# Later feed-forwards of a two-layer decoder trunk: a second pair of column groups through seven products, and another order of the matmuls in a group

## The chip, the cores and the metric

The kernel runs on one core of a Trainium2 chip, in one launch. The metric is the device time of a run in microseconds (us). One run of each kernel is taken by the hardware profiler; its span is the time from the first to the last instruction of the core, and the run's own time is a little longer than that.

## The reference, cut to what matters

Two layers work on 256 tokens of width 1024 in float32. Each layer is: a feed-forward, a token mixer, a second feed-forward, each followed by a layer norm. So there are four feed-forwards in all; the change is about these.

```python
def swiglu(x, w_gate, w_up, w_down):
    return (jax.nn.silu(x @ w_gate) * (x @ w_up)) @ w_down
...
D_FF = ((8 * D_MODEL // 3 + 127) // 128) * 128        # 2816
...
x = layer_norm(ALPHA * x + 0.5 * swiglu(x, ffn1_gate[l], ffn1_up[l], ffn1_down[l]), ln_g[l, 0], ln_b[l, 0])
```

## The kernel before, in words

**Precision.** Every float32 operand is split into a high part, rounded to the chip's fp32r type, and a low part, the rest. A product of two operands is three matmuls (high by high, high by low, low by high), which the helper `mm3` issues (line 120). A weight tile is 128 x 1024 (512 KB). It is loaded by one DMA on SyncE's (SP's) queue into a buffer named `raw`, of which there are five. ScalarE (ACT) casts it to `wh` (line 124), then VectorE (DVE) subtracts to get `wl` (line 125). Down-projection tiles go the same way and are called `dh`, `dl`. Gate and up tiles have eight buffers for `wh` and eight for `wl`; down tiles have six of each.

**Groups.** The 2816 hidden columns are cut into eleven groups, 0 to 10, of 256 gate and 256 up columns. A feed-forward is a hand-written list of steps (`FIRST` for the first feed-forward, `ORDER` for the three later ones), and TensorE (PE) works through it in that order:

- `G g.h`: group g for token half h; the tokens stand still in the array, and the weights stream through it. The product then has to be transposed on PE, by `T` (line 647), before it can be an operand of the down projection.
- `T g` in the list is the method `GT`: a *turned* group. The weights stand still and the tokens of both halves stream, 512 columns against `wh` (high and low tokens together) and 256 against `wl`, 64 matmuls (line 528). The result comes out already transposed. It needs four PSUM banks: two column blocks, each with a gate and an up bank. `gate_turned` adds the two sums of each bank and takes silu and product (lines 553 to 557).
- `D g.h`: the down projection of group g for token half h, 12 matmuls into `acc`.
- `A g.n` and `B g.n`, n = 0 to 3: a *summed pair*, groups g and g+1 with both token halves, as a two-by-two block product with seven products in place of eight (the Strassen-Winograd scheme). It needs sums of token blocks, `Sh` and `Sl`, made once per feed-forward, and sums of weight blocks: `first_sums` (line 237) and `later_sums` (lines 242 to 245) work in place on the `raw` tiles on DVE before they are split. A pair takes 14 weight tiles, where two turned groups take eight. After the last `B`, lines 481 to 493 make the four results u, p5, v (and c11, which is ready after `A`) on ACT and DVE, and each has to be transposed by `T`.

**What sets the order around the change.** PE's order is that of the program. ACT, DVE and SP orders are set by a scheduler; ops under `high_priority` move ahead. A small clock, `later`, counts products (three matmuls of 512 columns are one tick) and puts a transposition into PE's program after a number of ticks: those of a pair 5, 8, 10 and 11 ticks after its last `B` (`TURNS`). A `GT` and an `A g.0` begin with

```python
later.wait(lambda: not self.pending)
```

which issues all transpositions that are still pending at once, ahead of the group. PSUM banks named `gu` are four in all, shared by groups, pairs and transpositions in turn; where a turned group goes *by block* (`by_block`), its first eight k-steps write two banks only, and the other two are touched 16 matmuls later.

Of the kernel before, what the change touches and what calls it, by code (L numbers as in the profile page):

```python
# [19 lines left out]
S = 256  # L20
DEPTH = 2
KT = D // P
# [19 lines left out]
FIRST, ORDER = ([(STEPS[s[0]], *(int(n) for n in s[1:].split("."))) for s in steps.split()] for steps in (  # L42
# [4 lines left out]
FINAL = [s[1] for s in ORDER if s[0] == "D" and s[2] == 0][-3:-1]  # L47
SUMMED = 40
TURNS = (5,8,10,11)
PINNED, STARTED = 4, 4  # L50
HT = 8
# [34 lines left out]
def trunk(ctx: ExitStack, tc: tile.TileContext, t, out: bass.AP):  # L86
# [13 lines left out]
    later = Later()  # L100
# [17 lines left out]
    def mm3(ps, lh, ll, wh, wl, start, stop, more=False):  # L118
        for n, (a, b) in enumerate(((lh, wh), (lh, wl), (ll, wh))):
            nc.tensor.matmul(ps, a, b, start=start and n == 0, stop=stop and n == 2, skip_group_check=more)  # L120
        later.tick()

    def halves(dst_h, dst_l, src):
        first = nc.scalar.copy(dst_h, src)  # L124
        return first, nc.vector.tensor_tensor(dst_l, src, dst_h.bitcast(F32), ALU.subtract)  # L125
# [85 lines left out]
    def full_part(n, part, pt=None):  # L211

        own = scope[0].tile([P, 4, P], F32, name="cb", bufs=4)
        if pt:
            nc.scalar.copy(own, pt)
        else:
            ks = slice(4 * part, 4 * part + 4)
            nc.vector.tensor_tensor(own, xth[:, n, ks].bitcast(F32), xtl[:, n, ks].bitcast(F32), ALU.add)
        parts_seen[n, part] = own
        if len(parts_seen) == 1:  # L220
            sums[0] = [scope[0].tile([P, 4, KT // 2, P], F32R, name="S" + n) for n in "hl"]
        if (1 - n, part) in parts_seen:
            (a11, a12), (a21, a22) = ([parts_seen[i, part][:, k::2] for k in range(2)] for i in range(2))
            raw = rawp.tile([P, 4, 2, P], F32, name="raw")
            for dst, a, b, op in ((0, a21, a22, ALU.add), (2, a11, a21, ALU.subtract), (1, raw[:, 0], a11, ALU.subtract),
                                  (3, a12, raw[:, 1], ALU.subtract)):
                nc.vector.tensor_tensor(raw[:, dst], a, b, op)
            sh, sl = (s[:, :, 2 * part:2 * part + 2] for s in sums[0])
            halves(sh, sl, raw)
        if len(parts_seen) == 4:  # L230
            parts_seen.clear()
# [121 lines left out]
    class FFN:  # L353
# [155 lines left out]
        def GT(self, g):  # L509

            later.wait(lambda: not self.pending)
            ps = [[psg.tile([P, 2 * S], F32, name="gu") for _ in range(2)] for _ in range(2)]
            n = 0
            for lo in range(2):
                w = S if lo else 2 * S

                blocks = [[0], [1]] if lo or self.by_block(g) else [[0, 1]]
                for block in blocks:  # L520
                    for kt in range(KT):
                        later.wait(lambda: min(xT[0].done, xT[1].done) > kt)
                        weight = self.gw[g][kt // 2]
                        for i in block:
                            for part in range(2):
                                c = (kt % 2) * 512 + part * GW + i * P
                                x = xt2[:, kt].rearrange("p l h t -> p (l h t)")
                                nc.tensor.matmul(ps[i][part][:, 2 * S - w:], weight.parts[lo][:, c:c + P], x[:, 0:w],  # L528
                                                 start=kt == 0 and not lo, stop=kt == KT - 1 and lo == 1)
                                n += w  # L530
                                if n >= 3 * 512:
                                    n -= 3 * 512
                                    later.tick()
                        if kt % 2 and lo and block == [1]:
                            weight.uses = 1
                            weight.used()
                    if lo:
                        self.gate_turned(g, block[0], ps[block[0]])

        def by_block(self, g):  # L540
            return g == 8 or g == 2 and not self.first

        def turned(self, g):
            return (0 if self.first else 2) <= g < NG - 1 and not {g, g - 1} & self.pairs
# [30 lines left out]
        def start(self):  # L575
# [62 lines left out]
            for i in range(2):  # L638
                self.gate_turned(0, i, ps[i])
            for n in range(4):  # L640
                later(SUMMED + 4 * n, lambda n=n: full_part(n % 2, n // 2))
            self.GT(1)

        def T(self, g, hf, hn):
# [519 lines left out]
```

## Time and profile before

| what | value |
|---|---|
| three timed runs | 941.34, 943.33, 944.40 us (median 943.33) |
| the profiled execution: its own time, its span | 944.05 us, 942.3 us |
| PE matmul busy, PE weight load busy | 930.6 us (99%), 789.9 us (84%) |
| DVE busy, ACT busy | 742.5 us (79%), 545.9 us (58%) |
| the DMA queue of SP, share of 16 engines | 59.3% |
| granted TensorE clock over the span | 0.998 |

The profiled execution is 0.7 us over the median. A busy matmul includes time in the pipeline: one of 512 columns is shown as about 0.39 us, while the next one starts 0.23 us later. So PE's speed is read from starts, or from the chain of waits, whose pieces follow each other; a group of 64 matmuls is one piece there.

### The profile page before, as it was taken

How to read it: one execution, taken by the hardware profiler on the slowest of the kernel's cores; microseconds unless marked ns; L12 is line 12 of the kernel's file. 1: busy time of each engine (PE TensorE's matmuls, PEld its weight loads, DVE VectorE, ACT ScalarE, POOL GpSimd, SP SyncE). 2: the span in 40 equal slices, each digit the busy share in tenths (PEclk: the TensorE clock that was granted, in tenths of full speed). 3: DMA queues.
4: the chain of work that ended last, by engine and by line, in shares of the span. 5: the costliest groups of instructions: out<-in, count | busy, mean ns of one | idle time of the engine just before them, and what ended most of it. 6: DMA issues, size and time to landing. Idle time of an engine off the chain costs nothing.

```text
span 942.3 us, 13155 instructions
## 1 busy us (share of the span) xinstructions
PE 930.6 (99%) x4767; PEld 789.9 (84%) x4767; DVE 742.5 (79%) x1209; ACT 545.9 (58%) x840; POOL 23.0 (2%) x38
## 2 busy tenths in 40 slices
PE   9999999999999999999999999999999999999996
PEld 7878788888988888888888888888898888888885
DVE  7787978779979768986776589947899797689825
ACT  7765667368446754765446556743975466556720
POOL 0000000010010000000000000000000000000000
PEclk9999999999999999999999999999999999999999
DMA  8855798534525765897327568953417357469801
GB/s 303 317 197 167 261 344 290 194 99 135 207 85 194 270 207 180 288 320 237 128 97 248 175 210 307 329 208 101 139 63 268 111 191 251 167 217 310 317 1 45
DMA packets 55424, 192.62 MB, mean 204 GB/s; under 512 B 6592, under 2 KB 6848, under 8 KB 55360
## 3 DMA queue, kind: packets, MB, share of 16 engines
q1 hardware_dynamic: 55024, 191.14, 59.3%
q8 instruction: 37, 0.61, 0.3%
q0 software_dynamic: 192, 0.53, 0.2%
q14 instruction: 27, 0.22, 0.1%
q10 hardware_dynamic: 144, 0.13, 0.0%
HBM read 190.72 MB, written 1.05 MB: 204 GB/s over the span
## 4 chain that ended last, share of the span: by engine, by line
PE 83%; DVE 7%; DMA 7%; issue 2%; ACT 1%; SPq 0%; DVEq 0%; ACTq 0%
PE gu L120 26%; PE acc L120 26%; PE gu L528 23%; DMA raw<-in_gu 4%; DVE wl L125 2%; PE gu L1002 2%; DMA raw<-in_dn 2%; PE acc L928 1%; PE gu L202 1%; PE acc L874 1%; PE gu L647 1%; DVE hn L556 1%; DMA raw<-in_first 1%; DVE sil L554 0%; ACT wh L124 0%
## 5 line engine op out<-in xcount | busy, mean ns | idle before, releaser
L124 ACT CAST wh<-raw 128x1024 fp32r<-128x1024 f32 x252 | 263.4, 1053 | 169.0 <-DMA raw<-in_gu 61.0
L125 DVE TENSOR_TENSOR wl<-raw,wh 128x1024 fp32r<-128x1024 f32 x252 | 303.7, 1220 | 46.1 <-ACT wh L124 24.1
L120 PE MATMUL gu<-wh,xt 128*128 128x512 f32 x672 | 221.8, 393 | 0.0
L528 PE MATMUL gu<-xt,wh 128*128 128x512 f32 x800 | 187.2, 391 | 1.5 <-DVE sil L554 0.9
L528 PEld LDWEIGHTS gu<-xt,wh 128*128 128x128 f32 x800 | 149.7, 188 | 35.0 <-DVE htl L125 1.5
L120 PEld LDWEIGHTS gu<-wh,xt 128*128 128x128 f32 x672 | 126.0, 188 | 26.4 <-DVE xt L125 0.5
L120 PE MATMUL acc<-dh,hth 128*128 128x512 f32 x354 | 140.2, 396 | 0.0
L120 PE MATMUL acc<-dh,htl 128*128 128x512 f32 x354 | 138.1, 390 | 0.0
L120 PE MATMUL acc<-dl,hth 128*128 128x512 f32 x354 | 137.5, 388 | 0.0
L120 PE MATMUL gu<-wl,xt 128*128 128x512 f32 x336 | 131.1, 390 | 0.0
L125 DVE TENSOR_TENSOR dl<-raw,dh 128x1024 fp32r<-128x1024 f32 x88 | 105.7, 1219 | 23.8 <-ACT dh L124 23.5
L124 ACT CAST dh<-raw 128x1024 fp32r<-128x1024 f32 x88 | 92.0, 1051 | 36.1 <-DMA raw<-in_dn 32.3
L528 PEld LDWEIGHTS gu<-xt,wl 128*128 128x128 f32 x800 | 99.3, 192 | 2.0
L528 PE MATMUL gu<-xt,wl 128*128 128x256 f32 x800 | 99.8, 283 | 0.0
L120 PEld LDWEIGHTS acc<-dh,htl 128*128 128x128 f32 x354 | 66.4, 188 | 14.2
L120 PEld LDWEIGHTS acc<-dl,hth 128*128 128x128 f32 x354 | 66.6, 188 | 12.1
L120 PEld LDWEIGHTS acc<-dh,hth 128*128 128x128 f32 x354 | 66.6, 188 | 11.8
L120 PEld LDWEIGHTS gu<-wl,xt 128*128 128x128 f32 x336 | 63.2, 188 | 12.7
L554 DVE TENSOR_TENSOR sil<-gu,sil 128x256 f32<-128x256 f32 x50 | 20.9, 418 | 37.3 <-ACT sil L553 37.3
L564 ACT ACTIVATE sil<-gu 128x256 f32<-128x256 f32 x20 | 7.7, 383 | 41.7 <-PE gu L120 41.5
L124 ACT CAST hth<-hn 128x256 fp32r<-128x256 f32 x52 | 21.0, 406 | 16.7 <-DVE hn L556 16.0
L314 POOL TENSOR_TENSOR rs<-rs,neghalf 128x1 f32<-128x1 f32 x11 | 10.4, 949 | 741.9 <-DVE rs L313 741.9
(206 smaller groups left out, 1042.9 us busy)
## 6 DMA issues: line engine op xcount, KB each, us to landing
raw<-in_gu SPq DMA_DIRECT2D x196, 512.0 KB, 4.8
raw<-in_dn SPq DMA_DIRECT2D x88, 512.0 KB, 4.7
raw<-in_win SPq DMA_DIRECT2D x40, 512.0 KB, 4.5
raw<-in_wout SPq DMA_DIRECT2D x16, 512.0 KB, 5.0
lng<-in_ln_g SPq DMA_DIRECT2D x6, 512.0 KB, 6.7
lnb<-in_ln_b SPq DMA_DIRECT2D x6, 512.0 KB, 7.6
x<-in_first SPq DMA_DIRECT2D x4, 384.0 KB, 3.7
raw<-in_first SPq DMA_DIRECT2D x4, 384.0 KB, 5.8
```

The costliest lines, as they stand in the source:

```text
L120: nc.tensor.matmul(ps, a, b, start=start and n == 0, stop=stop and n == 2, skip_group_check=more)
L124: first = nc.scalar.copy(dst_h, src)
L125: return first, nc.vector.tensor_tensor(dst_l, src, dst_h.bitcast(F32), ALU.subtract)
L202: nc.tensor.transpose(pt[:, k - a, :], self.nat[:, k * P:(k + 1) * P], ident)
L314: nc.gpsimd.tensor_tensor(rs, rs, neghalf[:, 0:1], ALU.pow)
L528: nc.tensor.matmul(ps[i][part][:, 2 * S - w:], weight.parts[lo][:, c:c + P], x[:, 0:w], start=kt == 0 and not lo, stop=kt == KT - 1 and lo ...
L554: nc.vector.tensor_tensor(dst, p[:, 0:S], dst, ALU.add)
L556: nc.vector.tensor_tensor(h, h, gate, ALU.mult)
L647: nc.tensor.transpose(pt[:, i, :], hn[:, i * P:(i + 1) * P], ident)
L874: nc.tensor.matmul(pe[:, a:], lf[hf][c][:, h * P:(h + 1) * P], cumM[:, c, a:], start=True, stop=True)
L928: nc.tensor.matmul(dst[:, 2 * j:2 * j + 2, :], side[:, j, :], E[:, 2 * j:2 * j + 2, t0:t0 + dst.shape[2]], start=True, stop=True)
L1002: nc.tensor.matmul(ps[i // 2][:, i % 2, :], w, x, start=kt == 0 and n == 0 and i % 2 == 0, stop=kt == KT - 1 and n == 2 and i % 2 == 1)
```

## The change

In the three later feed-forwards, groups 6 and 7 were a summed pair and 5, 8 and 9 were turned. Now 5 and 6 are a pair and 8 and 9 are a second one, and 7 is turned and goes by block. Of the turned groups that do not go by block, the order of the 64 matmuls is new: the first four k-steps with `wh`, the same four with `wl`, then the other four with `wh` (all for both blocks), and last the other four with `wl`, block by block. Before, it was all eight with `wh`, then `wl` by block. In the first feed-forward the list of steps is the same, but its turned groups take the new order too, group 8 does not go by block any more, and the token sums are asked for later (66 ticks and every 6, before 40 and every 4).

```diff
-    "G0.0 G1.0 G0.1 G1.1 D0.0 D0.1 T2 D1.0 T3 D1.1 T4 D2.0 T5 D2.1 "
-    "A6.0 A6.1 A6.2 A6.3 D3.0 B6.0 D3.1 B6.1 D4.0 B6.2 B6.3 D4.1 D5.0 D5.1 T8 D6.0 D6.1 T9 D7.0 D7.1 D8.0 G10.0 D9.0 D10.0 G10.1 "))
+    "G0.0 G1.0 G0.1 G1.1 D0.0 D0.1 T2 D1.0 T3 D1.1 T4 D2.0 "
+    "A5.0 A5.1 A5.2 A5.3 D2.1 B5.0 D3.0 B5.1 D3.1 B5.2 B5.3 D4.0 D4.1 T7 D5.0 "
+    "A8.0 A8.1 A8.2 A8.3 D5.1 B8.0 D6.0 B8.1 D6.1 B8.2 B8.3 D7.0 D7.1 G10.0 D8.0 D9.0 D10.0 G10.1 "))
...
-SUMMED = 40
+SUMMED = 66
+EARLY = 4
...
-            for lo in range(2):
-                w = S if lo else 2 * S
-
-                blocks = [[0], [1]] if lo or self.by_block(g) else [[0, 1]]
-                for block in blocks:
-                    for kt in range(KT):
+            if self.by_block(g):
+                turns = [(lo, [i], 0, KT) for lo in range(2) for i in range(2)]
+            else:
+                turns = [(lo, [0, 1], 0, EARLY) for lo in range(2)] + [(0, [0, 1], EARLY, KT)]
+                turns += [(1, [i], EARLY, KT) for i in range(2)]
+            for lo, block, first, end in turns:
...
-                        if kt % 2 and lo and block == [1]:
+                        if kt % 2 and lo and 1 in block:
                             weight.uses = 1
                             weight.used()
-                    if lo:
+                    if lo and end == KT:
                         self.gate_turned(g, block[0], ps[block[0]])
 
         def by_block(self, g):
-            return g == 8 or g == 2 and not self.first
+            return g == 7 or g == 2 and not self.first
...
-                later(SUMMED + 4 * n, lambda n=n: full_part(n % 2, n // 2))
+                later(SUMMED + 6 * n, lambda n=n: full_part(n % 2, n // 2))
```

Three places of the built programs show what moves. Names carry the buffer number of the program; line numbers of the changed kernel are 2 to 4 higher.

The first place is PE in the last feed-forward, from the pair's last transpositions (`ident`) to the turned group behind it. Before, with pair 6 and 7 and group 8 (`acc` rows are down projections):

```order
L647 MATMUL gu_8650<-ident_88,cb_8425 128x128 x2
L120 MATMUL acc_7753<-dh_8413,hth_8225 128x512
L120 MATMUL acc_7753<-dl_8414,hth_8225 128x512
L120 MATMUL acc_7753<-dh_8413,htl_8226 128x512
L647 MATMUL gu_8660<-ident_88,cb_8582 128x128 x2
L120 MATMUL acc_7753<-dh_8419,hth_8294 128x512
L120 MATMUL acc_7753<-dl_8420,hth_8294 128x512
L120 MATMUL acc_7753<-dh_8419,htl_8295 128x512
L528 MATMUL gu_8682<-xt_86,wh_8455 128x512
```

Now, with pair 5 and 6 and group 7, where `cb_8449`, `cb_8295` and `cb_8450` are u, p5 and v:

```order
L122 MATMUL acc_7763<-dh_8289,hth_8176 128x512
L122 MATMUL acc_7763<-dl_8290,hth_8176 128x512
L122 MATMUL acc_7763<-dh_8289,htl_8177 128x512
L651 MATMUL gu_8497<-ident_88,cb_8449 128x128 x2
L651 MATMUL gu_8504<-ident_88,cb_8295 128x128 x2
L651 MATMUL gu_8511<-ident_88,cb_8450 128x128 x2
L532 MATMUL gu_8518<-xt_86,wh_8325 128x512
L532 MATMUL gu_8519<-xt_86,wh_8325 128x512
```

Three down projections stood between the pair and the turned group, now two; the last two transpositions, which the clock had put 10 and 11 ticks behind the pair, now stand directly ahead of the group, 8 ticks behind it.

The second place is DVE around the same results: `cb` is u, v and p5 at lines 484 to 487 and their products with silu at line 498. Before:

```order
L125 TENSOR_TENSOR wl_8492<-raw_8490,wh_8491 128x1024
L484 TENSOR_TENSOR cb_8582<-cb_8581,gu_8443 128x512
L485 TENSOR_TENSOR cb_8581<-cb_8581,gu_8318 128x512
L486 TENSOR_TENSOR cb_8425<-cb_8425,cb_8582 128x512
L125 TENSOR_TENSOR wl_8501<-raw_8499,wh_8500 128x1024
L498 TENSOR_TENSOR cb_8581<-cb_8581 128x256
L498 TENSOR_TENSOR cb_8425<-cb_8425 128x256
L487 TENSOR_TENSOR cb_8582<-cb_8582,gu_8444 128x512
L125 TENSOR_TENSOR dl_8507<-raw_8505,dh_8506 128x1024
L498 TENSOR_TENSOR cb_8582<-cb_8582 128x256
```

Now (lines 486 to 489 and 500):

```order
L486 TENSOR_TENSOR cb_8450<-cb_8449,gu_8313 128x512
L127 TENSOR_TENSOR dl_8383<-raw_8381,dh_8382 128x1024
L487 TENSOR_TENSOR cb_8449<-cb_8449,gu_8200 128x512
L488 TENSOR_TENSOR cb_8295<-cb_8295,cb_8450 128x512
L127 TENSOR_TENSOR wl_8410<-raw_8408,wh_8409 128x1024
L500 TENSOR_TENSOR cb_8449<-cb_8449 128x256
L500 TENSOR_TENSOR cb_8295<-cb_8295 128x256
L489 TENSOR_TENSOR cb_8450<-cb_8450,gu_8314 128x512
L127 TENSOR_TENSOR htl_8485<-gu_8481,hth_8484 128x256
L127 TENSOR_TENSOR wl_8419<-raw_8417,wh_8418 128x1024
L500 TENSOR_TENSOR cb_8450<-cb_8450 128x256
L239 TENSOR_TENSOR raw_8432<-raw_8432,raw_8408 128x512
```

Between the first of these results and the last product there stood two subtractions of weight tiles, now three, and the first transposition's `htl` besides.

The third place is PE in the first feed-forward at group 8. Before, by block, the group's 14th to 18th matmul:

```order
L528 MATMUL gu_1447<-xt_86,wh_1247 128x512
L528 MATMUL gu_1446<-xt_86,wh_1247 128x512
L528 MATMUL gu_1447<-xt_86,wh_1247 128x512
L528 MATMUL gu_1448<-xt_86,wh_1202 128x512
L528 MATMUL gu_1449<-xt_86,wh_1202 128x512
```

Now the last matmul ahead of the group and its first four:

```order
L122 MATMUL acc_483<-dh_1166,htl_1042 128x512
L532 MATMUL gu_1446<-xt_86,wh_1202 128x512
L532 MATMUL gu_1447<-xt_86,wh_1202 128x512
L532 MATMUL gu_1448<-xt_86,wh_1202 128x512
L532 MATMUL gu_1449<-xt_86,wh_1202 128x512
```

The banks `gu_1448` and `gu_1449`, which were first written by the 17th and 18th matmul, are now written by the third and fourth.

More of the change, by code (lines that the diff above doesn't have):

```diff
@@ L515, in GT @@
             n = 0
-            for lo in range(2):
-                w = S if lo else 2 * S
-                blocks = [[0], [1]] if lo or self.by_block(g) else [[0, 1]]
-                for block in blocks:
-                    for kt in range(KT):
+            if self.by_block(g):
[4 more added lines that the diff above has]
+            for lo, block, first, end in turns:
+                    w = S if lo else 2 * S
+                    for kt in range(first, end):
                         later.wait(lambda: min(xT[0].done, xT[1].done) > kt)
```

## The prediction

> **What bounds the kernel now.** I read the page's totals first, then the chain of waits, then the timelines of PE, VectorE and ScalarE around one summed pair.
>
> ```profile
> span 942.3 us, 13155 instructions
> PE 930.6 (99%) x4767; PEld 789.9 (84%) x4767; DVE 742.5 (79%) x1209; ACT 545.9 (58%) x840; POOL 23.0 (2%) x38
> PE 83%; DVE 7%; DMA 7%; issue 2%; ACT 1%; SPq 0%; DVEq 0%; ACTq 0%
> ```
>
> The chain runs on PE for 83% of the span. Its pieces in the last feed-forward (start, length, what):
>
> ```profile
> 822.58 11.11 PE gu L528 x64
> 833.69 2.74 PE acc L120 x12
> 836.43 8.19 PE gu L120 x36
> ...
> 847.37 2.77 PE gu L120 x12
> ...
> 852.89 2.75 PE gu L120 x12
> ...
> 858.40 5.47 PE gu L120 x24
> 863.87 3.43 PE acc L120 x15
> 867.30 0.22 PE gu L647 x2
> ...
> 872.06 0.22 PE gu L647 x2
> ```
>
> A turned group is 11.11 us, one D is 2.74, the four A steps are 8.19, the four B steps 2.77 + 2.75 + 5.47 = 10.99, one transposition 0.22. Piece follows piece: PE loses nothing here, so what leaves PE's list leaves the time, as long as its operands keep coming.
>
> **The PE work that goes.** Groups 8 and 9 turned cost 2 x 11.11 = 22.22 us. As a pair they cost 8.19 + 10.99 = 19.18, and four transpositions 4 x 0.22 = 0.88: 20.06 together. That saves 2.16 us in a feed-forward, 6.5 in three. Moving the first pair from 6 and 7 to 5 and 6 changes no count, and the new order inside a turned group issues the same 64 matmuls.
>
> **The work that comes on other engines.** VectorE's groups in that feed-forward (busy us, mean ns), and two stretches:
>
> ```profile
> L125 DVE TENSOR_TENSOR wl<-raw,wh 128x1024 fp32r<-128x1024 f32 x37 | 44.6, 1218 | 2.0 <-ACT wh L124 1.9
> L242 DVE TENSOR_TENSOR raw<-raw 128x512 f32<-128x512 f32 x4 | 2.7, 683 | 0.0
> L237 DVE TENSOR_TENSOR raw<-raw 128x512 f32<-128x512 f32 x4 | 2.6, 683 | 1.1 <-issue 1.1
> 836.00:873.00 37.00, 37.00 (x167) 30.18 (x166) 35.27 (x47) 22.90 (x31) 0.00 (x0) 1.00 0.84 283
> sum 128.00, PE 128.00 PEld 109.29 DVE 96.34 ACT 74.98 POOL 0.00; mean PE 42.67 PEld 36.43 DVE 32.11 ACT 24.99 POOL 0.00
> ```
>
> A second pair loads 14 tiles for 8. VectorE gets 6 x 1.22 = 7.3 us of subtractions and 16 weight sums of 0.68 = 10.9; the pair's own adds and products are about what two turned groups took. That is 18 us in each later feed-forward, 96.3 to about 114 of the 126 us that PE needs there. ScalarE gets six casts, 6.3 us, and SP six more DMAs; both have room (75 of 128 us; a DMA share of 0.84 at its highest). I cost the 18 us at nothing, because PE covers it. But in the stretch of the existing pair VectorE was busy 35.3 of 37 us (the fourth column). The cover there is thin, and that is where I look for the new wait.
>
> **The new wait.** Only two D steps now stand between the first pair and group 7. Count from the end of the pair's last B, which is the start of the next D:
>
> ```profile
> 863.71 0.39 PE L120 MATMUL acc<-dh,hth 128*128 128x512 f32 x1
> ...
> 871.90 0.38 PE L647 MATMUL gu<-ident,cb 128*128 128x128 f32 x2
> ...
> 872.81 0.39 PE L528 MATMUL gu<-xt,wh 128*128 128x512 f32 x1
> ```
>
> Before, the last transposition (of v) began 8.2 us after the pair. Now PE reaches it after 2 x 2.74 and three transpositions of 0.22, at 6.1 us. When is v's product there? VectorE's rows (start, length, what; in brackets its idle time and what ended it):
>
> ```profile
> 846.32 0.69 DVE L453 TENSOR_TENSOR cb<-cb,gu 128x512 f32<-128x512 f32 x1 [0.27 <-ACT cb L452]
> 847.27 1.22 DVE L125 TENSOR_TENSOR wl<-raw,wh 128x1024 fp32r<-128x1024 f32 x1 [0.26 <-ACT wh L124]
> ...
> 861.05 2.51 DVE L125 TENSOR_TENSOR wl<-raw,wh 128x1024 fp32r<-128x1024 f32 x2 [0.55 <-ACT wh L124]
> 863.99 1.23 DVE L125 TENSOR_TENSOR wl<-raw,wh 128x1024 fp32r<-128x1024 f32 x1 [0.42 <-ACT wh L124]
> 865.13 0.68 DVE L484 TENSOR_TENSOR cb<-cb,gu 128x512 f32<-128x512 f32 x1
> ...
> 867.12 1.22 DVE L125 TENSOR_TENSOR wl<-raw,wh 128x1024 fp32r<-128x1024 f32 x1
> ...
> 869.52 1.22 DVE L125 TENSOR_TENSOR dl<-raw,dh 128x1024 fp32r<-128x1024 f32 x1
> 870.66 0.42 DVE L498 TENSOR_TENSOR cb<-cb 128x256 f32<-128x256 f32 x1
> ```
>
> It ended at 870.66 + 0.42 = 871.08, 7.4 us after the pair, and nobody waited. The same in the second feed-forward, whose first transposition begins 15 matmuls (3.43 us) after the pair:
>
> ```profile
> 402.55 0.38 PE L647 MATMUL gu<-ident,cb 128*128 128x128 f32 x2
> 405.25 0.42 DVE L498 TENSOR_TENSOR cb<-cb 128x256 f32<-128x256 f32 x1 [0.45 <-ACT cb L497]
> ```
>
> 405.67 - 399.12 = 6.55 us. After the change the same product stands behind other subtractions. In the stream of tiles the first of the pair's A is number 1, and v's product follows number 25 before and number 26 now. Six of these were through VectorE when the turned group ahead of the pair ended; now I take seven, because the new order is through with that group's first two `wl` tiles after 5.6 of its 11.1 us, not in the last quarter, so that two more tiles of A can pass; one down tile fewer stands ahead. Nineteen remain both times, with the same sums in between: by work alone 7.4 us again, plus the `htl` that now stands ahead (as long as line 498's row, 0.42), 7.8. Below that, the idle rows above (0.27, 0.26, 0.55, 0.42) can close up, since two tiles are ahead: 6.3. I take 6.5, nearest to the second feed-forward's row, since the buffers are freed in time there as well. Then PE waits 6.5 + 0.1 - 6.1 = 0.5 us for v. Behind it the second matmul of group 7 needs the bank of the second transposition, which VectorE empties after one more sum (line 237, 0.68) and one `htl`, 1.1 us after v; PE would be there 0.6 us after v: another 0.5. So 1.0 us for each later feed-forward, 3.0 in all, from 0.8 x 3 at 6.3 to 2.3 x 3 at 7.8.
>
> The second pair has G10.0 behind its two D steps, so its transpositions keep their ticks; VectorE's list there has two subtractions between the first result and v's product, as before. I cost its wait at nothing; the cover is 8.2 against 7.4 us, and were it gone, the price is the difference. The moved loads of the layer norm's gains (1 MB on SP's queue) go behind the third tile of the next A; the tiles that v waits for are issued ahead of them, so nothing.
>
> **The first feed-forward.** Its PE work is unchanged. Two waits change:
>
> ```profile
> 62.90 1.29 PE L528 MATMUL gu<-xt,wh 128*128 128x512 f32 x4 [0.91 <-DVE sil L554]
> 58.37 1.22 DVE L125 TENSOR_TENSOR Sl<-raw,Sh 128x1024 fp32r<-128x1024 f32 x1
> 62.43 0.42 DVE L554 TENSOR_TENSOR sil<-gu,sil 128x256 f32<-128x256 f32 x1
> 127.43 1.11 PE L528 MATMUL gu<-xt,wh 128*128 128x512 f32 x4
> 127.95 0.75 DVE L125 TENSOR_TENSOR htl<-gu,hth 128x256 fp32r<-128x256 f32 x2
> 129.17 0.17 DVE L720 COPY pr<-lbs 128x8 f32<-128x8 f32 x1 [0.47 <-DMA lbs<-in_lb]
> ```
>
> At 62.90 group 4 waited 0.91 us for a bank that VectorE emptied late, behind the token sums (`Sl`). Half of these now come after that emptying: I take 0.5 saved, of 0 to 0.9. At 127.43 group 8 began while two transposition banks were full until 128.70; its third and fourth matmul, at 127.89 and 128.12, now write these: 0.6 us lost. The small copies that wait for `lbs` now stand ahead of these two rows, which could make it 2.4; the DMA is issued earlier too, so I stay at 0.6.
>
> **The sum.** -6.5 + 3.0 - 0.5 + 0.6 = -3.4 us. On the profiled execution's own 944.05 that is 940.6; on the median of 943.33 it is 939.9, 0.36% less, and I give 939.9. A difference under 0.3%, 2.8 us, can hardly be told from none in runs of this kernel.
>
> [...] The page's row has PE matmul 99% and weight load 84% busy. [...]
>
> **The rivals.**
>
> First, all hidden: v comes in time everywhere and group 7 waits 0.3 us for its bank; the rest as above. -6.5 + 0.9 + 0.1 = -5.5: 937.8. For it: VectorE's idle rows may close altogether. Against: 6.1 us is under every time that v took.
>
> Second, the wait eats the gain: v at 7.8 to 8.3. Then 2.3 to 2.8 us each: 6.9 to 8.4 less 6.4, +0.5 to +2.0, so 943.8 to 945.3. For it: the count by work alone gives 7.8. Against: the second feed-forward's 6.55.
>
> Third, slower: VectorE's stream becomes the bound. A tile's round through one of five `raw` buffers:
>
> ```profile
> raw<-in_gu SPq DMA_DIRECT2D x33, 512.0 KB, 4.7
> 861.25 1.05 ACT L124 CAST wh<-raw 128x1024 fp32r<-128x1024 f32 x1 [0.23 <-DMA raw<-in_gu]
> ```
>
> 4.7 to land, 1.05 to cast, 1.22 to subtract: 7.0 us for five tiles, 1.4 each. If the two tiles are not ahead, because the buffers and not the work set VectorE's pace, v comes 2 x 1.4 later than 7.4, at 10.2. The wait is then 4.2 + 0.5 in three places: 14.1 - 6.4 = +7.7, 951. It decides against the change as soon as v takes over 7.6 us, where the wait passes 2.16. Against it: the lead is in the order of the matmuls, and the DMA has room.
>
> **How the numbers follow.** The forecast has 0.45 (938 to 942), all hidden 0.15 (935.5 to 938), the gain eaten 0.25 (942 to 945.5), the stream as the bound 0.15 (946 to 951). Faster by over 0.3% means under 940.5: three quarters of the first (0.34) and all of the second, 0.49. Slower means over 946.2: 0.15. The rest is 0.36. The range leaves out the slow case and the outermost of the hidden one: 936 to 946.
>
> **What would show it.** After the change the chain should have pieces of 8.19 and about 11 us twice in each later feed-forward, and four pieces of 11.11 where there were six. Ahead of group 7 PE should show idle time ended by DVE at line 500, and at the group's second matmul by `htl`; over 2 us there would prove me wrong towards no gain. The last product should end about 6.5 us after the pair. Group 8 of the first feed-forward should wait 0.6 us at its third or fourth matmul. Waits for `wl` inside A or B would mean the third rival.

## The result, and the profile after

| | before | after |
|---|---|---|
| median of the runs | 942.92 us (4 runs) | 951.11 us (4 runs, 949.17 to 954.76) |
| ratio after to before | | 1.0089, 95% interval 1.0071 to 1.0107 |
| the profiled execution: its own time, its span | 944.05, 942.3 us | 951.94, 950.1 us |
| granted TensorE clock over the span | 0.998 | 0.995 |

The change made the kernel 8 us slower; 3.4 us faster was forecast. The page of after, totals and chain:

```profile
span 950.1 us, 13018 instructions
PE 930.1 (98%) x4659; PEld 781.9 (82%) x4659; DVE 794.2 (84%) x1266; ACT 558.9 (59%) x843; POOL 23.1 (2%) x38
PE 66%; DVE 17%; DMA 9%; issue 4%; ACT 3%; SPq 0%; DVEq 0%; ACTq 0%
```

The matmuls are fewer (4659 for 4767), VectorE has 51.7 us more (54 were counted), and the chain of waits runs on PE for 66% of the span where it was 83%. What PE waits for (line waited for: us in all, times, longest), before and then after (one row of 1.1 us for a tile `zero`, the same in both, and the smallest rows are left out):

```profile
PE gu L528 <- DVE sil L554: 0.9, 1, 0.9
PE gu L528 <- DVE htl L125: 0.4, 1, 0.4
```

```profile
PE gu L651 <- DVE cb L500: 4.5, 9, 1.2
PE gu L651 <- DVE hn L569: 4.2, 3, 2.0
PE gu L532 <- DVE sil L558: 0.8, 1, 0.8
PE gu L532 <- DVE htl L127: 0.8, 3, 0.3
```

Two new rows carry the loss: the pairs' products (line 500), and three times the product of G10.0 (line 569). Idle time in these rows begins at the end that the profile shows for a matmul (0.39 us behind its start, where the next one can start 0.23 behind), so it is about 0.17 us short each time (the wait of 2.04 us in the rows below is 2.21 by the starts on both sides). I therefore also count **lost spacing** from the starts of all matmuls: from one start to the next, what goes beyond 0.2285 us (512 columns), 0.119 (256) or 0.1 (128), other widths in proportion to 512 (the median spacings of before are 0.227, 0.120 and 0.109), summed over the span with its sign. It is 13.2 us before and 28.0 after. Without it the two spans are 929.0 and 922.2: PE's work fell by 6.9 us, and lost spacing rose by 14.7.

PE's rows at the second pair's transpositions of the second feed-forward, and at the first pair's last one and the turned group behind it in the last feed-forward:

```profile
437.40 0.38 PE L651 MATMUL gu<-ident,cb 128*128 128x128 f32 x2
441.12 0.44 PE L651 MATMUL gu<-ident,cb 128*128 128x128 f32 x2 [1.24 <-DVE cb L500]
443.19 0.44 PE L651 MATMUL gu<-ident,cb 128*128 128x128 f32 x2 [0.24 <-DVE cb L500]
451.43 0.44 PE L651 MATMUL gu<-ident,hn 128*128 128x128 f32 x2 [2.04 <-DVE hn L569]
...
863.57 0.44 PE L651 MATMUL gu<-ident,cb 128*128 128x128 f32 x2 [0.35 <-DVE cb L500]
864.50 1.88 PE L532 MATMUL gu<-xt,wh 128*128 128x512 f32 x7 [0.26 <-DVE htl L127]
```

By start spacing, the places cost in the three feed-forwards, in order: first pair and group 7 0.86, 1.88, 1.03 (3.8 us in all); second pair and G10.0 4.02, 2.73, 1.72 (8.5 us). With 1.5 us at a low clock, shown below, and 0.5 us less in the first feed-forward that is -6.9 + 3.8 + 8.5 + 1.5 - 0.5 = 6.4 of the 7.9 us between the spans; the rest is in many small differences. Times from the end of the last B, read from PE's and VectorE's rows:

| us after the pair | u's product | v's product | PE gets to u, v |
|---|---|---|---|
| before, pair 6 and 7 | 3.61, 5.10, 4.96 | 6.56, 7.50, 7.37 | 5.70, 8.19 |
| after, pair 5 and 6 | 3.68, 4.69, 3.85 | 6.41, 7.42, 6.59 | 5.70, 6.1 |
| after, pair 8 and 9 | 7.09, 6.03, 6.43 | 9.50, 8.44, 8.83 | 5.70, 8.2 |

Why the second pair is late stands in VectorE's rows of the last feed-forward, whose second pair ends at 905.66 (the row of 919.03 is ScalarE's):

```profile
906.31 2.52 DVE L127 TENSOR_TENSOR wl<-raw,wh 128x1024 fp32r<-128x1024 f32 x2 [0.58 <-ACT wh L126]
908.74 0.68 DVE L486 TENSOR_TENSOR cb<-cb,gu 128x512 f32<-128x512 f32 x1
909.34 1.22 DVE L127 TENSOR_TENSOR dl<-raw,dh 128x1024 fp32r<-128x1024 f32 x1
910.47 0.68 DVE L487 TENSOR_TENSOR cb<-cb,gu 128x512 f32<-128x512 f32 x1
...
912.60 1.22 DVE L127 TENSOR_TENSOR dl<-raw,dh 128x1024 fp32r<-128x1024 f32 x1
913.74 0.76 DVE L500 TENSOR_TENSOR cb<-cb 128x256 f32<-128x256 f32 x2
...
918.00 2.36 DVE L127 TENSOR_TENSOR dl<-raw,dh 128x1024 fp32r<-128x1024 f32 x2
919.03 0.38 ACT L568 ACTIVATE sil<-gu 128x256 f32<-128x256 f32 x1 [1.94 <-PE gu L122]
920.27 0.42 DVE L569 TENSOR_TENSOR hn<-sil,gu 128x256 f32<-128x256 f32 x1
```

The first result (line 486) begins 3.1 us after the pair; before, its like began 1.4 after (865.13 less 863.71). In the two feed-forwards ahead of this one it begins 3.7 and 2.7 us after the second pair, and before 0.1 and 1.6 after the pair. Two subtractions for group 10 stand ahead of it in the queue, and they came late themselves (0.58 idle for ScalarE's cast). At the end the product of G10.0 could begin at 919.4, when ScalarE's silu ended, and the two subtractions of D10's tiles in row 918.00, which nobody needs yet, hold it to 920.27.

A last part of the loss is the clock. PE (first figure behind the length) and its granted clock (third from the right) in the wait at 451, behind it, and later:

```profile
449.00:451.40 2.40, 0.39 (x2) 0.00 (x0) 1.92 (x4) 1.81 (x3) 0.00 (x0) 1.00 0.96 326
453.30:456.30 3.00, 3.00 (x9) 2.36 (x8) 1.90 (x2) 1.05 (x1) 0.00 (x0) 0.51 0.99 340
457.00:460.00 3.00, 3.00 (x15) 2.46 (x14) 0.94 (x2) 0.00 (x0) 0.00 (x0) 1.00 0.77 292
```

From 452.8 on, 1.4 us behind the end of the wait, the clock is at half for 3.4 us, and eight matmuls stand 0.43 us apart: 1.5 us lost on top of the wait.

### The profile page after: what moved, and what is told of

It is laid out like the page before. It is cut to its first block, busy times and chain, and to the rows that moved or that the text cites. A ratio compares the mean times of both kernels' runs of the same rounds, so it can differ in the third digit from the quotient of the medians.

```text
span 950.1 us, 13018 instructions
## 1 busy us (share of the span) xinstructions
PE 930.1 (98%) x4659; PEld 781.9 (82%) x4659; DVE 794.2 (84%) x1266; ACT 558.9 (59%) x843; POOL 23.1 (2%) x38
## 4 chain that ended last, share of the span: by engine, by line
PE 66%; DVE 17%; DMA 9%; issue 4%; ACT 3%; SPq 0%; DVEq 0%; ACTq 0%
PE gu L122 23%; PE acc L122 19%; PE gu L532 16%; DMA raw<-in_gu 7%; DVE wl L127 6%; DVE dl L127 3%; PE gu L1006 2%; ACT wh L126 1%; DMA raw<-in_dn 1%; PE acc L932 1%; DVE raw L247 1%; DVE htl L127 1%; PE gu L204 1%; PE acc L878 1%; DVE cb L500 1%
## 5 line engine op out<-in xcount | busy, mean ns | idle before, releaser
L126 ACT CAST wh<-raw 128x1024 fp32r<-128x1024 f32 x270 | 280.6, 1053 | 191.6 <-DMA raw<-in_gu 52.0
L127 DVE TENSOR_TENSOR wl<-raw,wh 128x1024 fp32r<-128x1024 f32 x270 | 325.4, 1222 | 41.9 <-ACT wh L126 30.5
L122 PE MATMUL gu<-wh,xt 128*128 128x512 f32 x744 | 249.8, 394 | 0.0
L532 PE MATMUL gu<-xt,wh 128*128 128x512 f32 x608 | 145.8, 392 | 1.8 <-DVE sil L558 0.8
L532 PEld LDWEIGHTS gu<-xt,wh 128*128 128x128 f32 x608 | 112.8, 188 | 26.9 <-DVE sil L558 1.8
L532 PEld LDWEIGHTS gu<-xt,wl 128*128 128x128 f32 x608 | 77.2, 191 | 2.5
L532 PE MATMUL gu<-xt,wl 128*128 128x256 f32 x608 | 77.9, 283 | 0.0
L122 PE MATMUL gu<-wl,Sh 128*128 128x512 f32 x112 | 43.8, 391 | 0.0
L122 PE MATMUL gu<-wh,Sh 128*128 128x512 f32 x112 | 43.8, 391 | 0.0
L122 PE MATMUL gu<-wh,Sl 128*128 128x512 f32 x112 | 43.6, 390 | 0.0
```

## The experiments

Theories at the start: *volume*, VectorE's work is the bound around the pairs; *cover*, the work fits but the transpositions stand too close behind a pair; later a third, *order*, the results stand behind subtractions in VectorE's queue that nobody needs yet. Ratios are to runs of before on the same chip; "lost" is the lost spacing of the profiled run (before 13.2, after 28.0), "DVE" VectorE's busy time there. The edits are shortened: `...` and comments stand for code that is left out.

| run | median us | ratio (95%) | lost | DVE |
|---|---|---|---|---|
| e1 old step list, rest new | 948.59 | 1.0054 (1.0038, 1.0071) | 17.3 | 743.3 |
| e2 new step list, rest old | 954.40 | 1.0123 (1.0105, 1.0141) | 31.4 | 793.3 |
| e3 second pair turned later | 953.15 | 1.0102 (1.0089, 1.0115) | 29.7 | 794.0 |
| e4 no sums, second pair | 947.35 | 1.0044 (1.0027, 1.0061) | 19.8 | 765.5 |
| e5 sums on GpSimd | 978.65 | 1.0369 (1.0355, 1.0382) | 55.1 | 780.0 |
| e6 six raw buffers | 957.33 | 1.0146 (1.0133, 1.0159) | 31.1 | 791.2 |
| e7 pairs farther apart | 955.00 | 1.0122 (1.0107, 1.0137) | 28.2 | 793.5 |
| e8 the same, more cover | 954.69 | 1.0113 (1.0091, 1.0134) | 33.3 | 792.9 |
| e9 results first | 954.09 | 1.0118 (1.0101, 1.0134) | 29.2 | 792.9 |
| e10 e9, banks by ScalarE | 952.06 | 1.0092 (1.0074, 1.0110) | 26.6 | 792.8 |
| e11 first feed-forward only | 942.41 | 0.9991 (0.9982, 1.0000) | 11.1 | 742.4 |
| e12 no sums in the later ones | 940.90 | 0.9973 (0.9963, 0.9983) | 17.9 | 737.7 |
| e13 e1, banks by ScalarE | 944.04 | 1.0012 (1.0003, 1.0021) | 12.8 | 743.9 |
| e14 pair 5 and 6 alone | 948.78 | 1.0058 (1.0045, 1.0070) | 18.0 | 742.7 |
| e15 e10, six raw buffers | 954.99 | 1.0146 (1.0120, 1.0172) | 28.3 | 790.7 |
| e16 all results first | 945.12 | 1.0027 (1.0011, 1.0043) | 23.4 | 791.8 |
| e17 e16, G10.0 turned later | 942.97 | 1.0008 (0.9990, 1.0026) | 19.2 | 791.6 |
| e18 e17, D9's tiles ahead | 945.07 | 1.0018 (1.0003, 1.0032) | 19.3 | 791.7 |

**The parts of the change: e1, e2, e11, e14, e13.**

e1, after with the old `ORDER` (and `by_block` for group 8 of the later feed-forwards, as that list needs):

```diff
-    "... T4 D2.0 A5.0 ... D4.1 T7 D5.0 A8.0 ... D7.1 G10.0 D8.0 D9.0 D10.0 G10.1 "
+    "... T5 D2.1 A6.0 ... D4.1 D5.0 D5.1 T8 D6.0 D6.1 T9 D7.0 D7.1 D8.0 G10.0 D9.0 D10.0 G10.1 "
```

> The step list of before (one pair, 6 and 7), with everything else of the change: the new order in the turned groups, group 8 of the first feed-forward not by block, the later token sums. Volume theory (VectorE's stream of two pairs is too long for the places where PE waits for it) and cover theory (the stream fits, but the transpositions stand too close behind the pair): both 942 to 943.5, as before, since both put the loss on the second pair. Third possibility, the loss is in the new order inside the groups: 946 or more.

5 us slower without any second pair, which the third possibility had and neither theory. VectorE's rows, and PE's at group 8 of the third feed-forward:

```profile
590.53 0.42 DVE L126 TENSOR_TENSOR htl<-gu,hth 128x256 fp32r<-128x256 f32 x1
590.87 2.35 DVE L126 TENSOR_TENSOR wl<-raw,wh 128x1024 fp32r<-128x1024 f32 x2
593.13 0.41 DVE L126 TENSOR_TENSOR htl<-gu,hth 128x256 fp32r<-128x256 f32 x1
```

```profile
593.60 3.74 PE L531 MATMUL gu<-xt,wh 128*128 128x512 f32 x15 [1.57 <-DVE htl L126]
```

Two subtractions of the tiles that the new order lets in earlier stand between two `htl`, and PE waits 1.6 us for the bank that the second `htl` empties.

e2, after with the old order of matmuls in a group, and the old sums and group 8 in the first feed-forward:

```diff
-                turns = [(lo, [0, 1], 0, EARLY) for lo in range(2)] + [(0, [0, 1], EARLY, KT)]
-                turns += [(1, [i], EARLY, KT) for i in range(2)]
+            turns = ... [(0, [0, 1], 0, KT)]
+            turns += [(1, [i], 0, KT) for i in range(2)]
...
-SUMMED = 66
+SUMMED = 40
...
```

> The new step list alone: turned groups in the old order, sums and group 8 of the first feed-forward as before. Both theories: about 951, and up to 1.4 us more in each later feed-forward if the early release of two tiles had helped the pair, so 951 to 955. If the new order inside the groups costs the time: 944 to 946.

As expected, 954.4. With two pairs the new order helps (3.3 us between the medians, of which the first feed-forward's part, in this run as before, is some 0.9 by e11), but it moves the wait more than it takes it: the places at group 7 cost 9.1 us here (3.8 in after), those at the second pair 3.3 (8.5).

e11, e1 with the old order of matmuls in the later feed-forwards too:

```diff
-            if self.by_block(g):
-                turns = [(lo, [i], 0, KT) for lo in range(2) for i in range(2)]
+            if not self.first:
+                turns = [(0, [i], 0, KT) for i in range(2)] if self.by_block(g) else [(0, [0, 1], 0, KT)]
+                turns += [(1, [i], 0, KT) for i in range(2)]
```

> The step list of before and the old order inside the turned groups of the later feed-forwards; of the change only what concerns the first feed-forward is left (its turned groups in the new order, group 8 not by block, later token sums). In the kernel with the old list and everything else new, the first feed-forward ended 1.3 us earlier than before and the later three lost 5.3. If the new order inside the groups is what lost them: 941 to 942.5. If it was the disturbed first feed-forward that carries on: 945 or more.

942.4: the new order inside the groups is what e1 lost (6 us). What is left, the first feed-forward's part, is a gain of 0.1%, and of the versions with the whole computation this is the only one whose ratio lies under 1 (interval up to 1.0000).

e14, after with pair 5 and 6 alone:

```diff
-    "A8.0 A8.1 A8.2 A8.3 D5.1 B8.0 D6.0 B8.1 D6.1 B8.2 B8.3 D7.0 D7.1 G10.0 D8.0 D9.0 D10.0 G10.1 "
+    "D5.1 T8 D6.0 D6.1 T9 D7.0 D7.1 D8.0 G10.0 D9.0 D10.0 G10.1 "
```

> After, with the first pair (5 and 6) alone: group 7 turned by block behind it, 8 and 9 turned; PE's work as before the change, 6.5 us more than after. If the second pair makes VectorE too late: none of its 8.5 us of waits, those at group 7 stay at 1 us or less each: 942 to 946. If the place of the first pair with two D steps behind it is what costs: 948 or more.

948.8, as the case in which the first pair's place costs: 1.5, 2.2 and 1.5 us at group 7 (`cb` at line 498, then `htl`), and 1.6 once at group 4. So in steps: first feed-forward -0.9, first pair's place and the order in the groups +6.4, second pair +2.3 (2.9 by the ratios), where it saves PE 6.9. The parts act on each other: the place at group 7 costs 5.2 us with one pair, 3.8 with two.

e13, e1 with ScalarE emptying the banks of the pair's transpositions:

```diff
             with tc.high_priority(offset=AHEAD):
+                nc.scalar.copy(spare, pt)       # spare: the free half of cb
+                pt = spare
                 halves(hth, htl, pt)
```

> The old step list with the new order inside the groups (948.6 us; PE waited 1.74, 1.73 and 0.26 us for htl at the second matmul of group 8), and ScalarE copies each transposed result of the pair out of its bank, so that group 8 does not wait for VectorE. If htl behind two subtractions is the loss: those 3.7 us and the low clock behind them go, 943 to 945. If the tiles come late: the wait moves to wl or wh in group 8, 947 to 949.

4.5 of the 6 us came back, and no wait over 0.6 is left in the later feed-forwards. The low clock that is expected here behind e1's waits is not in e1's profile: its granted clock is 1.00 in each of four stretches up to 930 us. So most of e1's loss is `htl` behind subtractions; the 1.6 us between this run and e11 stay unexplained.

**Cover or volume: e3, e4, e12, e5, e6, e7, e8.**

e3:

```diff
+            late = 0 if self.first or g != 8 else 4
-                self.turn(slots, n, hf, c[:, GW:])
+                self.turn(slots + late, n, hf, c[:, GW:])
-            slots = {(NG - 1, 0): 2, (NG - 1, 1): 4}
+            slots = {(NG - 1, 0): 2 if self.first else 6, (NG - 1, 1): 4}
```

> After, but the second pair's four transpositions come 4 ticks (2.7 us) later and that of G10.0 too (6 ticks behind it instead of 2), so they lie between or behind the matmuls of G10.0, D8.0 and D9.0. Cover theory: the 8.5 us of waits of the second pair and the 1.6 us at low clock go, 941 to 943. Volume theory: PE only meets the same late VectorE in D8.0 to D10.0, 948 to 951.

953.2, over both ranges, and cover alone falls: PE waits 3.1 and 3.6 us at D8.0 instead.

e4 and e12 leave sums out (e4: `cut` is the second pair's first tile; e12: every tile of the later feed-forwards):

```diff
-                    how = lambda raw: later_sums(raw, None)
+                    how = None if n >= cut else lambda raw: later_sums(raw, None)
```

> After, without the 16 sums of weight blocks of the second pair in each later feed-forward (that part of the computation is left out), 10.9 us less on VectorE, all of it ahead of the second pair's results. Volume theory: the second pair's waits go, 941 to 943. Cover theory, or a stream that is held by the raw buffers and not by work: the tail from the last B to G10.0 holds no sums and stays as it is, 948 to 951.

> After, without the 16 sums of weight blocks of either pair in the three later feed-forwards (that part of the computation is left out): 22 us of VectorE less in each, under what before has there. Volume theory: the waits of the first pair go as well as those of the second, 935 to 938. Order theory: VectorE's queue still has the subtractions ahead of the small operations, 1 to 2 us at each T7 stay: 940 to 944.

e4: 947.4, between the two ranges. In its profile, of its fastest run, the second pair's waits went from 8.5 to 0.6 us, and those at group 7 rose to 5.9. The tail itself holds no sums, so what VectorE did earlier had made it late. Whether that is VectorE's work as such, or the time for which a sum holds a `raw` buffer, this run can't tell: with a sixth buffer (e6) these waits go as well, and no sum is taken away. e12: group 7's waits are gone as well, but two of G10.0's stay, although VectorE has less to do than before the change:

```profile
PE 927.4 (99%) x4659; PEld 781.9 (83%) x4659; DVE 737.7 (78%) x1170; ACT 561.0 (60%) x843; POOL 22.7 (2%) x38
```

```profile
PE gu L652 <- DVE hn L570: 2.6, 2, 1.6
```

So volume is not all: 935 to 938 was expected, 940.9 measured.

e5, the second pair's sums with `nc.gpsimd` for `nc.vector`:

```diff
-                    how = lambda raw: later_sums(raw, None)
+                    how = lambda raw, eng=eng(n): later_sums(raw, None, eng)
```

> After, but the 16 sums of weight blocks of the second pair run on GpSimd instead of VectorE; nothing is left out. Volume theory (VectorE's work is the bound there): like the run without these sums, 943 to 947. Rival: GpSimd takes much longer than 0.68 us for a sum, or holds VectorE up while it reads, and the tiles of the pair come late: waits for wh or wl inside A8 or B8, 951 to 965.

```profile
L247 POOL TENSOR_TENSOR raw<-raw 128x512 f32<-128x512 f32 x12 | 23.2, 1938 | 0.9
```

```profile
L127 DVE TENSOR_TENSOR wl<-raw,wh 128x1024 fp32r<-128x1024 f32 x170 | 213.9, 1274 | 36.5 <-ACT wh L126 34.2 <-PE gu L534 1.8
```

978.7, over the rival's range too. A sum takes 1.6 to 1.9 us there for 0.69, the ten summed tiles of the pair wait for it before their cast, the pairs' products come late (14.3 us of PE's waits end there), and VectorE's own subtractions grew from 1221 to 1274 ns. This run does not separate what a sum takes on GpSimd by itself from what comes of both engines being at work.

e6:

```diff
-RAW, NW, ND = 5, 8, 6
+RAW, NW, ND = 6, 8, 6
-HT = 8
+HT = 6
```

> After, with six raw buffers for five (room for it comes from HT = 6 for 8, the buffers of transposed products). If the stream is held by the round through the raw buffers (VectorE idle 10 us of the 95 around the two pairs, ended by ScalarE behind a DMA): VectorE's idle closes, the second pair's waits go from 8.5 to 2 or 3 us, 944 to 946. If VectorE's work is the bound: 949 to 952; more if the transposed products now wait for buffers.

957.3, over both ranges. The second pair's waits fell to 0.9 us, as the buffer idea has it, but group 7's second matmul now waited 2.95, 2.47 and 2.96 us for `htl`: two subtractions, ready sooner, stood ahead of it.

e7 and e8 (pairs 4 and 5, 8 and 9, with group 6 by block; e8 moves one D from inside each pair to behind it):

```diff
-    "... T4 D2.0 A5.0 ... B5.3 D4.0 D4.1 T7 D5.0 A8.0 ... "
+    "... T3 D1.1 A4.0 ... B4.3 D3.1 T6 D4.0 D4.1 T7 D5.0 A8.0 ... "
```

> After, with the first pair one group earlier: groups 4 and 5, then 6 and 7 turned, then 8 and 9 as before; the same work on every engine, two turned groups between the pairs for one. A turned group takes PE 11.1 us and VectorE 8.3 (4 subtractions of 1.22, 8 small operations of 0.42), so VectorE catches up 2.8 us more before the second pair. Volume theory: the second pair's 1.7 to 4.0 us of waits in a feed-forward fall to 0 to 1, that behind the first pair stays: 943 to 946. Cover theory: the second pair is as it was, 950 to 952.

> As the spread kernel (pairs 4 and 5, 8 and 9), and one D step moved from inside each pair to behind it, so that three stand between the last B and the turned group or G10.0. Cover theory: both places of waiting go, 938 to 941. Volume theory: the tiles inside the pair come later than PE, so the waits move into B (wl), and the time is that of the spread kernel or up to 3 us more: 944 to 949.

955.0 and 954.7, which neither theory had. In e7 the waits changed place and kept their sum: 1.5 us left at the second pair, 10.5 at group 6 (12.3 in after). In e8 the sum grew to some 15.5 us: group 6 waits for nothing, but the first pair's transpositions 2.9, the first matmuls of A and B 3.7, G10.0's transposition 3.1 and 3.0, and the rest is at the second pair.

**Order: e9, e10, e15, e16, e17, e18.** No part of the computation is taken away here; ordering edges are added in VectorE's queue, in e16 to e18 in ScalarE's too, and from e10 on ScalarE also makes the copies of e13.

e9:

```diff
+                for n in (2, 3):        # of the weight tiles that follow the pair
+                    if later_w[n].parts:
+                        tc.add_manual_dep(later_w[n].second.ins, behind.ins.name, NoSync)
```

> After, with VectorE's order alone changed: the subtractions of the last two of the four weight tiles that follow a pair (group 7's, group 10's) must stand behind the last sum of the pair's results (v); no work is added or taken. Order theory (the results are late because subtractions of 1.22 us that nobody waits for yet stand ahead of them in VectorE's queue): two subtractions less ahead of the second pair's results, its waits go from 8.5 to 2 to 4 us, 944 to 947. Volume theory: what is put behind comes late itself, as waits for wl in G10.0 or in the group, 950 to 952.

The results came early (second pair's v at 6.1 to 7.6 us after the pair, it was 8.4 to 9.5) and the time did not fall (954.1, over both ranges). The waits went to the next small operation behind a subtraction:

```profile
PE gu L659 <- DVE hn L577: 6.6, 3, 3.1
PE gu L540 <- DVE htl L127: 5.9, 3, 2.1
```

e10 adds e13's copy to this:

> As the kernel with the results first, and ScalarE also copies each transposed result of a pair out of its PSUM bank (into the half of cb that is free by then), so that the bank no longer waits for VectorE's htl. Order theory: the waits for htl at the second matmul of group 7 (0.51, 0.52, 0.51 in after) go too, 1 to 2 us less than the kernel with the results first, 943 to 945. Volume theory: no change, 950 to 952.

Group 7 waits for nothing now; 11 us are left at the second pair, most for `hth` and `hn`.

e15 is e10 with e6's six buffers:

> Both pairs, the results first in VectorE's queue, banks emptied by ScalarE, and six raw buffers (HT 6). If VectorE's idle time behind DMAs is what is left of the loss: the 14 us of waits of the kernel with five buffers (952.1) fall by 6 or more, 942 to 946. If VectorE's work is: 949 to 953.

No gain, 955.0, over both ranges: a sixth raw buffer doesn't take away what is left. (The buffers of transposed products went from 8 to 6 with it; what that costs was not run by itself.)

e16 is e10 with edges for the down tiles of D9 and D10 as well:

```diff
+                        if o.parts:      # o: the tiles of D9 and D10
+                            behind(o.first, first)     # ScalarE: cast behind the last hth
+                            behind(o.second, second)   # VectorE: behind the last htl
...
+                            behind(o.second, mul)      # and behind G10.0's product
```

> As the kernel with the results first and banks emptied by ScalarE (952.1 us), and the down tiles of D9 and D10 are cast and subtracted only behind the second pair's last transposed result and G10.0's product. Order theory: the waits for hth and for hn there (9 to 11 us in three feed-forwards) go, 941 to 944, and the pair begins to pay. Volume theory: the four down tiles are late in their turn and PE waits for dl in D9.0 or D10.0, 949 to 953.

7 us less than e10, with the same work; the range of the order theory ended 1 us lower. The largest of PE's waits that is left:

```profile
PE gu L670 <- DVE hn L583: 4.1, 3, 1.5
```

e17:

```diff
+            late = int(g == 8 and not self.first)      # one tick more for p5 and v
...
-            slots = {(NG - 1, 0): 2, (NG - 1, 1): 4}
+            slots = {(NG - 1, 0): 2 if self.first else 5, (NG - 1, 1): 4}
```

> As the kernel with all results first (945.1 us), with G10.0's transposition 5 ticks behind it instead of 2 (inside D9.0), and the second pair's p5 and v one tick later. If only their place is short: the three waits of 1.5 us at G10.0's transposition and those of 0.4 at p5 go, 939 to 941, under before and under the kernel with the first feed-forward's part alone (942.4). If the stream is late: PE waits for dl in D9.0 or for htl in D10.0 instead, 944 to 946.

942.97, level with before, and between the two ranges. That row is gone, and this one has come; beside it VectorE's row where it stands idle ahead of the product:

```profile
PE acc L122 <- DVE dl L127: 3.2, 3, 1.2
```

```profile
911.66 0.42 DVE L584 TENSOR_TENSOR hn<-sil,gu 128x256 f32<-128x256 f32 x1 [1.82 <-ACT sil L583]
```

e18 lets the subtractions of D9's tiles into that gap:

```diff
-                for n in (9, 10):
+                for n in (10,):
```

> As the last kernel (942.97 us), but the subtractions of D9's two down tiles may go ahead of G10.0's product, in the 1.8 us in which VectorE stood idle there. Order theory: the three waits of 1.0 to 1.3 us for dl in D9.0 go and none comes in their place, 939 to 940.5. Volume theory: G10.0's product and its transposition are late by as much, 942 to 944.

945.07, over both ranges. The wait moved to D10.0:

```profile
PE acc L122 <- ACT hth L126: 3.8, 2, 1.9
```

For a comparison the first 200 us are best left out: e17 and e18 have the same edits for the first feed-forward, yet their profiles lose 2.7 and 5.2 us there (waits of 2 us at 47 to 51 us are in one and not in the other). Behind 200 us the lost spacing is 23.6 us in after, 23.0 in e10, 17.8 in e16, 16.4 in e17, 14.0 in e18, 13.9 in e12 without any sums, and 8.4 before.

What follows from all: of the 14.7 us of new lost spacing about 9 (28.0 to 19.2) go with every part of the computation kept, by three things together: what PE needs next stands first in VectorE's *and* ScalarE's queues (e16), ScalarE empties the banks (e10, which ends the waits at group 7), and G10.0's transposition stands later (e17). At one place alone the new order only moved the wait (e9). Less work shrinks the waits too, without any reordering (e4, e12). The rest over before stayed in e17 and e18, at different places; whether it would go with less work or with one more reordering stays open, since no run had both. Why e18's median is 2 us over e17's, with less lost behind 200 us in its profile, is open too; its granted clock was 0.995 or 0.996 in 7 of 12 runs, e17's in one.

## Why the prediction was wrong

**The step that failed** is "I cost its wait at nothing; the cover is 8.2 against 7.4 us" for the second pair. It cost 8.5 us, and 1.5 at low clock. The 7.4 us was carried over from the existing pair with the count of subtractions between the first result and v's product, and that count held: two, here as there. What I did not count was where the first result starts: 3.1 us after the pair instead of 1.4, behind the four subtractions of the next group, which came late. That the second pair starts without the lead that the first pair has used up is the likely reason: with two turned groups between the pairs in place of one (e7) 1.5 us of the 8.5 are left. And the start of the results is not all of it: e9 brought them early and the time did not fall, as `htl` and G10.0's product then waited behind the subtractions. And "its transpositions keep their ticks" was true of the pair's four but forgot a fifth, G10.0's, 2 ticks behind that group, whose product stands behind the subtractions of the down tiles: 4.7 of the 8.5 us.

**VectorE's 18 us**, "at nothing, because PE covers it", was the same error one step earlier. I compared sums over a feed-forward (114 of 126 us). From the last turned group ahead of the first pair to G10.0, 826 to 921 us in after, VectorE is busy 85.0 of 95 us, and its twelve operations at the first pair (856.29 to 863.43) stand in the order of the program; this row is its last stretch, behind the second pair (third figure, 14.32 of 15):

```profile
906.00:921.00 15.00, 13.77 (x65) 10.45 (x63) 14.32 (x20) 10.07 (x17) 0.00 (x0) 1.00 0.52 193
```

**The new wait at group 7** came as written: v at 6.41, 7.42 and 6.59 us (6.5 taken), idle ended by line 500 and at the second matmul by `htl`, 3.8 us for 3.0. As a price of the first part it was too small: alone (e14) that place costs 5.2, and 1.6 more came at group 4.

**The order in a group** was costed at a lead of one tile, a help. With two pairs it is one (e2). With one pair it costs 6 us (e1 against e11), 4.5 of them through a queue position and not through work (e13).

**PE's saving**, 6.5 us, was 6.9, and 608 matmuls of turned groups stand against `wh` where 800 did, six groups less. **The first feed-forward**: for +0.1 it gained 0.5 us of lost spacing in after (4.8 to 4.3 in the first 200 us), 0.9 us in e11's runs. Of its two terms, the wait at 62.90 went wholly; 0.84 came at 49.02, a place that cost between nothing (e17) and 2 us (e18) in runs with the same edits there, so the 0.5 us is within that scatter; group 8's 0.6 did not come at all:

```profile
126.92 3.36 PE L532 MATMUL gu<-xt,wh 128*128 128x512 f32 x14
```

**The rivals.** The third, slower at 951, had the time and the resource, the time by luck: it put the waits at group 7 with 4.7 us each, where 1.3 was lost. I gave it 0.15 on the ground that the two tiles' lead is in the order of the matmuls. At the second pair that lead was gone. Its sign, waits for `wl` inside A or B, did not come: VectorE kept the tiles in time, and was late with everything small.

## What to carry to other kernels

A stage that saves the bounding engine work and gives it to a helper is to be costed where the helper's queue stands at that moment: when does it *begin* the first result, and which long operations that nobody needs yet are ahead of each small one that somebody does. Sums over a whole phase hide that, and so does a count that starts at the first result. When a wait is removed and the time stays, look at the next small operation behind a long one in the same queue (here e9 to e18); one place put right may only move the wait (e9).

## What was not expected of the hardware

The forecast has no term for the clock behind a wait. In after, the wait of 2.04 us that ended at 451.43 was followed, from 452.8 on, by 3.41 us at a granted clock of half, with matmuls of 512 columns 0.43 us apart instead of 0.23. Not every wait of that length had this behind it: in e10 PE waited 2.75 us until 448.52, and its matmuls stand 0.23 us apart for the 3.4 us that follow, but for the next wait of 0.27. In e9 two waits of 2.1 us differ. PE's busy time is the first figure behind the length, the granted clock the third from the right:

```profile
391.20:394.60 3.40, 1.29 (x6) 0.97 (x6) 3.40 (x6) 0.17 (x1) 0.00 (x0) 1.00 0.95 327
394.60:398.00 3.40, 3.40 (x10) 2.61 (x9) 2.25 (x4) 1.52 (x2) 0.00 (x0) 0.50 0.93 336
575.50:578.90 3.40, 2.88 (x16) 2.17 (x14) 3.40 (x7) 2.25 (x6) 0.00 (x0) 1.00 0.45 155
578.90:582.30 3.40, 1.81 (x8) 1.52 (x9) 3.40 (x7) 0.00 (x0) 0.00 (x0) 1.00 0.97 345
582.30:585.70 3.40, 3.40 (x17) 2.82 (x16) 2.24 (x3) 2.19 (x3) 0.00 (x0) 1.00 0.98 372
```

In the first two rows PE stands without a matmul for 2.11 us, and then has half the clock for 3.4 us. In the last three it stands for 0.52 and 1.59 us, and has the full clock throughout. Why one wait had it and the other not, these runs do not show.

Over the whole span, the granted clock of the profiled run was 0.989 to 0.996 in after, e2, e3, e5 to e9 and e15, and 0.997 or 0.998 in the eleven others. These nine are also the nine with 28.0 us of lost spacing or more, part of which is the low clock itself. In e4's runs the time goes along with the clock: 944.05 us at 0.998, 948.97 and 949.95 at 0.992.
